# Norm roots taken out of the first FFN products behind two mixers

## The chip, the cores and the metric

The kernel runs on one core of one Trainium2 chip. The metric is device time of one execution in microseconds, median over the timed runs. The engines are TensorE (PE: matmuls; PEld: its weight loads), VectorE (DVE), ScalarE (ACT), GpSimd (POOL) and SyncE (SP, which issues most transfers). Each engine works through its own list of instructions in order.

## The reference

Two layers. Each is half a SwiGLU feed-forward network (FFN), a token mixer (layer 0: a grouped 2-D Fourier transform and a projection; layer 1: retention), and a second half FFN. D is 1024, the FFN is 2816 wide, there are 256 latent and 256 context tokens. Layer 1's mixer updates the latent stream only, so its second FFN has 256 tokens.

```python
def rmsnorm(x, g):
    y = xf * lax.rsqrt(jnp.mean(xf * xf, axis=-1, keepdims=True) + NORM_EPS)
    return (y * g).astype(x.dtype)

def half_ffn(t, m, j):
    h = modulate(rmsnorm(t, norm_g[l, j]), m[3 * j], m[3 * j + 1])   # h * (1 + scale) + shift
    return t + 0.5 * m[3 * j + 2] * swiglu(h, w_gate, w_up, w_down)  # (silu(h @ gate) * (h @ up)) @ down

x = half_ffn(x, m_lat, 0);  ctx = half_ffn(ctx, m_ctx, 0)
y_lat, y_ctx = fourier_layer(...)            # layer 0; retention_layer in layer 1
x = x + m_lat[5] * y_lat;   ctx = ctx + m_ctx[5] * y_ctx
x = half_ffn(x, m_lat, 2);  ctx = half_ffn(ctx, m_ctx, 2)
```

The root of the norm is one number per token; scale and shift are one number per feature.

## The kernel before

Activations stand transposed: features on the 128 partitions, tokens along the row. `x_tile(d, s)` is feature block d (0 to 7) of stream s (0 latent, 1 context), 128x256. To keep float32 precision each operand of a product is a pair, hi (rounded) and lo (the rest); `split` makes it with a cast on ACT (L89) and a subtraction on DVE (L90), and `mm3` issues three matmuls (L132 to L134) for a product. Weight blocks come by DMA as 128x2048 `raw` tiles and are split in two halves (`wh`, `wl`, 128x1024 each), in order, on ACT and DVE.

The FFN works on blocks i of 128 of its 2816 columns: for a block, gate and up each sum 8 products over k (the feature blocks) in one PSUM bank. There are six such banks (`ps`, 128x512). `hidden` evicts a pair: silu on ACT (L437), product on DVE (L439), a split.

Between a mixer and the FFN behind it stands the norm. `square` squares an updated x tile on ACT (L271) and adds it to a running sum (L278: POOL in the Fourier layer, DVE in retention; with `apart=2` the last two tiles are not added). `rstd` sums the sums over the partitions with one-column matmuls (L303), takes the root (ACT L308), its inverse (DVE L310), puts it on a diagonal (L312) and spreads it over the partitions with a matmul (L319). `keep_warm` (L250) issues matmuls whose results are unused, at these points. `norm_mod` then makes the pair of the normed input, per d: x times scale times root on DVE (L335), hi with the shift on ACT (L336), lo on DVE (L337). Only behind these can the FFN's first product start.

In the Fourier layer the last stage (`fourier`, L654 on) goes over the 8 feature blocks d: 24 products plus one matmul of 256 or 258 columns, a copy on ACT (L667), three combinations on DVE (L676 to L678) and the two residual updates of x on DVE (L369), then the squares. `begin_two` starts the FFN that follows with two blocks: latent products of block 0, then of block 1, then the context products of both while norm_mod works on them, and from the third block on the streams go together, 512 columns wide. In retention the last `project_out` ends with the residual updates of the latent tiles, and `begin_narrow` starts the last FFN with blocks 0 and 1, 256 columns wide.

`behind(d)` and `tc.issue_after(x)` only set the order on one engine: what stands in them is put behind the named instruction. All other order on an engine comes from a planner which replays the program with its own durations and lists the instructions by when they would be ready.

Of the kernel before, what the change touches and what calls it, by code (L numbers as in the profile page):

```python
# [16 lines left out]
P = 128  # L17
# [14 lines left out]
GRID_W = 64  # L32


@with_exitstack
def hybrid_block(ctx: ExitStack, tc: tile.TileContext, a: dict, out: bass.AP):
# [44 lines left out]
    def h_tile():  # L81
        return hpool.tile([P, 512], F32R, tag="h", name=nm("h"))
# [170 lines left out]
    sums = {}  # L253

# [13 lines left out]
    def square(d, s, eng=nc.gpsimd, apart=0):  # L268

        sq = q_tile()  # L270
        nc.scalar.activation(sq, x_tile(d, s), AF.Square)  # L271
        if d == 0:
            sums[s] = [sq]
        elif d >= ND - apart:
            sums[s].append(sq)
        else:
            n = q_tile()
            eng.tensor_tensor(n, sums[s][0], sq, ALU.add)  # L278
            sums[s] = [n]
# [44 lines left out]
    def h_tiles():  # L324
        return [(h_tile(), h_tile()) for _ in range(ND)]

    def norm_mod(l, j, s, h, r):
        sl = STREAMS[s]
        done, acts = [], []
        for d in range(ND):  # L330
# [3 lines left out]
            with tc.issue_after(done[d - 3].ins) if d > 2 else nullcontext():  # L334
                nc.vector.scalar_tensor_tensor(u, x_tile(d, s), sc, r, ALU.mult, ALU.mult)  # L335
# [16 lines left out]
    def rstd_tokens():  # L352

        ps = aux_tile()
        for s in range(2):
# [6 lines left out]
        root = spool.tile([P, 4], F32, tag="root4", bufs=1, name=nm("root"))  # L362
        mark[2] = nc.scalar.activation(root, ps[:, :4], AF.Sqrt, bias=epst[:, 1:2])
        inv = spool.tile([P, 4], F32, tag="inv4", bufs=1, name=nm("inv"))
# [64 lines left out]
    def half_ffn(l, j, h, width, begin, after, each=None):  # L429
        f = 2 * l + j // 2  # L430
        off = 0
        for c0, c1 in CHUNKS:
            hid = []

            def hidden(psg, psu):
                sg = t_tile()
                mark[1] = nc.scalar.activation(sg[:, :width], psg[:, :width], AF.Silu)  # L437
                hf = t_tile()
                nc.vector.tensor_tensor(hf[:, :width], psu[:, :width], sg[:, :width], ALU.mult)  # L439
                uh, ul = a_tile(), a_tile()  # L440
                split(uh[:, :width], ul[:, :width], hf[:, :width])
                hid.append((uh, ul))
# [124 lines left out]
    def fourier(l, slot, after):  # L567
# [84 lines left out]
        four["last"] = mark[0], mark[6]  # L652

        for b in range(4):  # L654
# [5 lines left out]
            for d in (2 * b, 2 * b + 1):  # L660
# [18 lines left out]
                for s in range(2):  # L679
                    residual(d, z[:, STREAMS[s]], l, 5, s)  # L680
                    square(d, s, nc.gpsimd, 2)
                    if d == ND - 1 and s == 0:
                        sqrt_table()
                        keep_warm(NW[0], mark[4])
                        after(0)
        after(1)
# [23 lines left out]
    def retention(l, slot, h, mid, after):  # L710
# [220 lines left out]
        def project_out(hd, zt, between=None, behind=None):  # L931
            for half in range(2):
                blk = wblock(a["ret_out"][slot, hd, half], 2048)
                for dd in range(4):
# [7 lines left out]
                    if hd == HEADS - 1:  # L942
                        square(d, 0, nc.vector, 2)
# [4 lines left out]
        for hd in range(HEADS):  # L948
# [39 lines left out]
            else:  # L988
                project_out(hd - 1, zts.pop(0), turn, mark[4].ins)
        project_out(HEADS - 1, zts.pop(0))  # L990
        keep_warm(NW[0], mark[4])
        after(0)
# [11 lines left out]
    def prepare(l, j, width, warm=False):  # L1004
# [16 lines left out]
        return after  # L1021

# [85 lines left out]
    def begin_narrow(load, bank, part, hidden):  # L1108
        blks, banks = [load(0), load(1)], [(bank(), bank()) for _ in range(2)]
        with behind(ND - 1):  # L1110
            pre = [load(2)]
        for k in range(ND):
            for i, gu in ((0, 0), (0, 1), (1, 0)):
                part(blks[i], banks[i][gu], gu, (k,), STREAMS[0])
        part(blks[1], banks[1][1], 1, range(ND), STREAMS[0])
        for i in range(2):
            hidden(*banks[i])
        return 2, pre

# [20 lines left out]
    fourier(0, 0, prepare(0, 2, T2, True))  # L1140
    half_ffn(0, 2, nxt["h"], T2, begin_two, prepare(1, 0, T2))
    half_ffn(1, 0, nxt["h"], T2, begin_two, prepare(1, 1, T2))
    retention(1, 0, nxt["h"], late, prepare(1, 2, S, True))
    half_ffn(1, 2, nxt["h"], S, begin_narrow, finish, scale_out)
# [98 lines left out]
```

## Time and profile before

| | us |
|---|---|
| timed runs, median (lowest to highest of 3) | 1656.64 (1655.84 to 1658.22) |
| the profiled execution, own time | 1658.49 |
| its span, first to last instruction | 1656.7 |
| PE busy in it | 1627.9 |
| DVE busy | 1130.2 |
| ACT busy | 626.8 |
| POOL busy | 122.2 |

Times below are microseconds from the span's start. A row of the time line has start, duration, engine, line, operation, output<-inputs, tile shapes and xcount; in brackets the idle time of the engine ahead of it and what ended it. Matmuls are pipelined, so the distance of two starts is the cost of one, not its duration.

### The profile page before, as it was taken

How to read it: one execution, taken by the hardware profiler on the slowest of the kernel's cores; microseconds unless marked ns; L12 is line 12 of the kernel's file. 1: busy time of each engine (PE TensorE's matmuls, PEld its weight loads, DVE VectorE, ACT ScalarE, POOL GpSimd, SP SyncE). 2: the span in 40 equal slices, each digit the busy share in tenths (PEclk: the TensorE clock that was granted, in tenths of full speed). 3: DMA queues.
4: the chain of work that ended last, by engine and by line, in shares of the span. 5: the costliest groups of instructions: out<-in, count | busy, mean ns of one | idle time of the engine just before them, and what ended most of it. 6: DMA issues, size and time to landing. Idle time of an engine off the chain costs nothing.

```text
span 1656.7 us, 23275 instructions
## 1 busy us (share of the span) xinstructions
PE 1627.9 (98%) x9352; PEld 1422.9 (86%) x9352; DVE 1130.2 (68%) x1805; ACT 626.8 (38%) x910; POOL 122.2 (7%) x192
## 2 busy tenths in 40 slices
PE   6999999999999999999999999999999999999998
PEld 4788888888998888888988888888988999999998
DVE  5588889887866776766567767733666767665554
ACT  4531222345542122223432222233564454354443
POOL 0011011023200000001200000001100000000000
PEclk9999999999999999999999999999999999999999
DMA  9576776752235444544144444522133333345451
GB/s 333 227 269 209 244 258 223 252 189 95 77 140 179 168 165 153 197 162 167 70 153 177 160 161 164 185 90 100 71 127 128 127 112 143 127 165 190 168 189 53
DMA packets 59740, 272.03 MB, mean 164 GB/s; under 512 B 7537, under 2 KB 8945, under 8 KB 41969
## 3 DMA queue, kind: packets, MB, share of 16 engines
q1 hardware_dynamic: 40512, 201.86, 34.5%
q0 software_dynamic: 18576, 68.17, 11.6%
q8 instruction: 73, 1.20, 0.3%
q10 hardware_dynamic: 544, 0.52, 0.1%
q14 instruction: 35, 0.28, 0.1%
HBM read 265.27 MB, written 5.24 MB: 163 GB/s over the span
## 4 chain that ended last, share of the span: by engine, by line
PE 96%; DVE 2%; DMA 1%; ACT 1%; issue 0%; SPq 0%; DVEq 0%; ACTq 0%
PE ps L132 31%; PE ps L133 31%; PE ps L134 31%; DMA a<-in_ada_first 1%; PE ps L764 0%; DMA xctx<-in_x 0%; PE aux L250 0%; PE aux L303 0%; PE aux L195 0%; ACT wh L89 0%; PE aux L319 0%; PE aux L925 0%; DVE a L90 0%; PE ps L839 0%; DVE xlat L369 0%
## 5 line engine op out<-in xcount | busy, mean ns | idle before, releaser
L89 ACT CAST wh<-raw 128x1024 fp32r<-128x1024 f32 x344 | 352.5, 1031 | 713.8 <-PE ps L133 624.0
L133 PE MATMUL ps<-h,wh 128*128 128x512 f32 (+1 forms) x1568 | 556.0, 356 | 0.0
L134 PE MATMUL ps<-h,wl 128*128 128x512 f32 (+1 forms) x1568 | 554.9, 355 | 0.0
L132 PE MATMUL ps<-h,wh 128*128 128x512 f32 (+1 forms) x1568 | 551.1, 356 | 3.6 <-ACT h L89 3.4
L90 DVE TENSOR_TENSOR wl<-raw,wh 128x1024 fp32r<-128x1024 f32 x344 | 410.1, 1197 | 181.2 <-ACT wh L89 177.9
L132 PEld LDWEIGHTS ps<-h,wh 128*128 128x128 f32 x1568 | 294.3, 189 | 46.1 <-ACT h L89 4.0
L133 PEld LDWEIGHTS ps<-h,wh 128*128 128x128 f32 x1568 | 297.1, 190 | 42.1 <-DVE h L90 0.5
L134 PEld LDWEIGHTS ps<-h,wl 128*128 128x128 f32 x1568 | 297.1, 190 | 41.4
L222 DVE CUSTOM_DVE_ANT_0 dump<-araw,wide,adab 128x1024 bf16<-128x1024 f32 x256 | 329.4, 1287 | 3.2
L134 PE MATMUL ps<-a,wl 128*128 128x512 f32 (+2 forms) x952 | 317.5, 336 | 0.0
L132 PE MATMUL ps<-a,wh 128*128 128x512 f32 (+2 forms) x952 | 317.4, 336 | 0.0
L133 PE MATMUL ps<-a,wh 128*128 128x512 f32 (+2 forms) x952 | 317.4, 336 | 0.0
L133 PEld LDWEIGHTS ps<-a,wh 128*128 128x128 f32 x952 | 180.5, 190 | 18.6
L134 PEld LDWEIGHTS ps<-a,wl 128*128 128x128 f32 x952 | 180.5, 190 | 18.4
L132 PEld LDWEIGHTS ps<-a,wh 128*128 128x128 f32 x952 | 179.5, 190 | 18.6
L439 DVE TENSOR_TENSOR t<-ps,t 128x512 f32<-128x512 f32 (+1 forms) x88 | 54.9, 624 | 177.6 <-PE ps L134 149.2
L213 POOL DMA_DIRECT2D araw<-in_ada_w x128 | 67.7, 529 | 828.0 <-DVE mods L222 783.5
L369 DVE SCALAR_TENSOR_TENSOR xlat<-ps,mods,xlat 128x256 f32<-128x256 f32 x128 | 61.1, 481 | 63.6 <-PE ps L134 63.0
L437 ACT ACTIVATE t<-ps 128x512 f32<-128x512 f32 (+1 forms) x88 | 47.9, 545 | 132.7 <-PE ps L134 127.1
L90 DVE TENSOR_TENSOR a<-t,a 128x512 fp32r<-128x512 f32 (+2 forms) x116 | 69.8, 606 | 2.6 <-ACT a L89 2.2
L89 ACT CAST a<-t 128x512 fp32r<-128x512 f32 (+2 forms) x116 | 64.3, 558 | 13.7 <-DVE t L868 9.8
L278 POOL TENSOR_TENSOR q<-q,q 128x256 f32<-128x256 f32 x52 | 46.8, 917 | 177.6 <-ACT q L271 177.1
(208 smaller groups left out, 1142.2 us busy)
## 6 DMA issues: line engine op xcount, KB each, us to landing
raw<-in_wgu SPq DMA_DIRECT2D x85, 1024.0 KB, 4.8
araw<-in_ada_w POOLq DMA_DIRECT2D x128, 512.0 KB, 3.9
raw<-in_wd SPq DMA_DIRECT2D x32, 896.0 KB, 4.5
raw<-in_ret_in SPq DMA_DIRECT2D x24, 1024.0 KB, 4.7
raw<-in_wd SPq DMA_DIRECT2D x16, 1024.0 KB, 4.8
a<-in_ada_first SPq DMA_DIRECT2D x32, 256.0 KB, 5.2
t<-in_four_w SPq DMA_DIRECT2D x32, 256.0 KB, 5.4
raw<-in_ret_out SPq DMA_DIRECT2D x8, 1024.0 KB, 4.7
```

Source lines behind the costliest of these rows:

```text
L89: mark[6] = nc.scalar.copy(hi, src)
L90: i = (lo_eng or nc.vector).tensor_tensor(lo, src, f32(hi), ALU.subtract)
L132: nc.tensor.matmul(ps, lh, rh, start=start, stop=False)
L133: nc.tensor.matmul(ps, lh, rl, start=False, stop=False)
L134: mark[4] = nc.tensor.matmul(ps, ll, rh, start=False, stop=stop)
L213: nc.gpsimd.dma_start(raw, a["ada_w"][l, m, d])
L222: nc.vector.tensor_tensor_reduce(dump, raw, wide[:, v, :], 1.0, adab[:, l, m, d : d + 1], ALU.mult, ALU.add, mods[l][:, m, d, v : v + 1],)
L278: eng.tensor_tensor(n, sums[s][0], sq, ALU.add)
L369: mark[0] = nc.vector.scalar_tensor_tensor(x_tile(d, s), ps, mods[l][:, m, d, s : s + 1], x_tile(d, s), ALU.mult, ALU.add)
L437: mark[1] = nc.scalar.activation(sg[:, :width], psg[:, :width], AF.Silu)
L439: nc.vector.tensor_tensor(hf[:, :width], psu[:, :width], sg[:, :width], ALU.mult)
```

## The change

The FFN behind each mixer starts with products of x times its scale, not of the normed input. The root, one factor per token, is multiplied in when a PSUM bank is evicted (`evict`), and the shift, which the root must not touch, goes through the same matmuls as two extra columns in front of the 256 token columns (`SH = 2`): each h tile is 16 columns longer, and the shift columns stand in columns 14 and 15, the tokens from column 16. `open` fills the shift columns (POOL), `tile(d)` makes the pair of x times scale (ACT, DVE) right behind the latent residual of d, `roots` makes the roots of both streams at once. Behind the Fourier layer block 0 and block 1 of the latent stream are made so (`products`, 258 columns); the context stream and all later blocks take the normed input as before. Behind retention it is blocks 0, 1 and 2. The squares are now all added, all on POOL, and in the Fourier layer they are issued behind both residuals of d, context first. The keep-warm matmuls at both places go. Weight block 1 (behind retention 1 and 2) is split only behind the last `tile` and the last square. All tiles of the pool have the longer form; who else uses them sees them from column 16.

```diff
+SH = 2
+PAD = 16
...
     def h_tile():
-        return hpool.tile([P, 512], F32R, tag="h", name=nm("h"))
+        return hpool.tile([P, PAD + T2], F32R, tag="h", name=nm("h"))
...
-        nc.scalar.activation(sq, x_tile(d, s), AF.Square)
+        squared[0] = nc.scalar.activation(sq, x_tile(d, s), AF.Square)
...
-    def rstd_tokens():
+    def rstd_tokens(n=2, scale=1.0):
         ps = aux_tile()
-        for s in range(2):
+        for s in reversed(range(n)):
...
         four["last"] = mark[0], mark[6]
+        following.open()
...
-                    square(d, s, nc.gpsimd, 2)
-                    if d == ND - 1 and s == 0:
-                        sqrt_table()
-                        keep_warm(NW[0], mark[4])
-                        after(0)
-        after(1)
+                    if s == 0:
+                        following.tile(d)
+                for s in (1, 0):
+                    square(d, s)
+        sqrt_table()
...
-                        square(d, 0, nc.vector, 2)
+                        following.tile(d)
+                        square(d, 0)
...
+        following.open()
         project_out(HEADS - 1, zts.pop(0))
-        keep_warm(NW[0], mark[4])
-        after(0)
...
+    class Ahead:
+        def __init__(self, l, j):
+            self.l, self.j = l, j
+        def open(self):
+            need(self.l, 3 * self.j + 1)
+            self.full = [(h_tile(), h_tile()) for _ in range(ND)]
+            nxt["h"] = [(hi[:, PAD:], lo[:, PAD:]) for hi, lo in self.full]
+            self.full = [(hi[:, PAD - SH :], lo[:, PAD - SH :]) for hi, lo in self.full]
+            nxt["done"] = [], []
+            for d, (hi, lo) in enumerate(self.full):
+                sh = mods[self.l][:, 3 * self.j, d, 0:1].broadcast_to([P, SH])
+                nc.gpsimd.tensor_copy(hi[:, :SH], sh)
+                nc.gpsimd.tensor_tensor(lo[:, :SH], sh, f32(hi[:, :SH]), ALU.subtract)
+        def tile(self, d):
+            sc = mods[self.l][:, 3 * self.j + 1, d, 0:1]
+            hi, lo = (t[:, STREAMS[0]] for t in nxt["h"][d])
+            nxt["done"][1].append(nc.scalar.activation(hi, x_tile(d, 0), AF.Copy, scale=sc))
+            mark[0] = nc.vector.scalar_tensor_tensor(lo, x_tile(d, 0), sc, f32(hi), ALU.mult, ALU.subtract)
+            nxt["done"][0].append(mark[0])
+        def products(self, blk, ps, k):
+            hi, lo = (t[:, : SH + S] for t in self.full[k])
+            for gu in range(2):
+                mm3(
+                    ps[gu][:, : SH + S], wcols(blk, k // 4 * 1024 + gu * 512 + k % 4 * P, P), (hi, lo),
+                    k == 0, k == ND - 1,
+                )
+        def evict(self, ps, r):
+            col = spool.tile([P, 2], F32, tag="col", name=nm("col"))
+            v = []
+            for gu in range(2):
+                nc.vector.tensor_copy(col[:, gu : gu + 1], ps[gu][:, 0:1])
+                v.append(q_tile())
+                nc.vector.tensor_tensor(v[gu], ps[gu][:, SH : SH + S], r, ALU.mult)
+            return v, col
+        def gate(self, v, col, pair):
+            uh, ul = pair
+            sg = q_tile()
+            mark[1] = nc.scalar.activation(sg, v[0], AF.Silu, bias=col[:, 0:1])
+            hf = q_tile()
+            nc.vector.scalar_tensor_tensor(hf, v[1], col[:, 1:2], sg, ALU.add, ALU.mult)
+            split(uh[:, :S], ul[:, :S], hf)
+        def roots(self, n):
+            inv = rstd_tokens(n, 1.0 / D**2)
+            diag = t_tile()[:, : n * S]
+            nc.vector.tensor_tensor(
+                diag.rearrange("p (a b) -> p a b", b=P), ident.unsqueeze(1).broadcast_to([P, 2 * n, P]),
+                inv.unsqueeze(2).broadcast_to([P, 2 * n, P]), ALU.mult,
+            )
+            r = aux_tile()
+            for s in range(n):
+                nc.tensor.matmul(r[:, STREAMS[s]], meanw, diag[:, STREAMS[s]], start=True, stop=True)
+            row = q_tile()
+            nc.scalar.copy(row, r[:, :S])
+            return r, row
+        def begin_two(self, load, bank, part, hidden):
+            late = STREAMS[1]
+            h = nxt["h"]
+            blks, lat = [load(0)], [(bank(), bank()) for _ in range(2)]
+            with behind(ND - 1), tc.issue_after(squared[0].ins):
+                blks.append(load(1))
+            for k in range(ND):
+                self.products(blks[0], lat[0], k)
+                if k == 5:
+                    r, row = self.roots(2)
+            nxt["done"] = norm_mod(self.l, self.j, 1, h, r[:, late])
+            with behind(3):
+                first = self.evict(lat[0], row)
+            for k in range(ND):
+                self.products(blks[1], lat[1], k)
+            with behind(ND - 1):
+                second = self.evict(lat[1], row)
+                pre = [load(2)]
+            ctx = [(bank(), bank()) for _ in range(2)]
+            for k in range(ND):
+                for i in range(2):
+                    for gu in range(2):
+                        part(blks[i], ctx[i][gu], gu, (k,), late)
+                if k == 0:
+                    with tc.issue_after(mark[0].ins), tc.issue_after(mark[6].ins):
+                        nxt["done"] = norm_mod(self.l, self.j, 0, h, r[:, :S])
+            pairs = [(a_tile(), a_tile()) for _ in range(2)]
+            with behind(ND - 1):
+                self.gate(*first, pairs[0])
+                self.gate(*second, pairs[1])
+                for i in range(2):
+                    hidden(*ctx[i], pairs[i], late)
+                pre.append(load(3))
+            return 2, pre
+        def begin_narrow(self, load, bank, part, hidden):
+            n = 3
+            h = nxt["h"]
+            blks, lat = [load(0)], [(bank(), bank()) for _ in range(n)]
+            with behind(ND - 1), tc.issue_after(squared[0].ins):
+                blks += [load(i) for i in range(1, n)]
+            for k in range(ND):
+                self.products(blks[0], lat[0], k)
+                if k == 4:
+                    r, row = self.roots(1)
+            first = self.evict(lat[0], row)
+            h[:] = [(hi[:, S:], lo[:, S:]) for hi, lo in h]
+            with tc.issue_after(mark[0].ins), tc.issue_after(mark[6].ins):
+                nxt["done"] = norm_mod(self.l, self.j, 0, h, r[:, :S], slice(0, S), range(5))
+            with behind(4):
+                pre = [load(n)]
+            with tc.issue_after(mark[0].ins), tc.issue_after(mark[6].ins):
+                done = norm_mod(self.l, self.j, 0, h, r[:, :S], slice(0, S), range(5, ND))
+            nxt["done"] = tuple(i + j for i, j in zip(nxt["done"], done))
+            for i in range(1, n):
+                for k in range(ND):
+                    self.products(blks[i], lat[i], k)
+            with behind(ND - 1):
+                pre.append(load(n + 1))
+                for ready in [first] + [self.evict(ps, row) for ps in lat[1:]]:
+                    pair = a_tile(), a_tile()
+                    self.gate(*ready, pair)
+                    hidden(None, None, pair, None)
+            return n, pre
...
-    fourier(0, 0, prepare(0, 2, T2, True))
-    half_ffn(0, 2, nxt["h"], T2, begin_two, prepare(1, 0, T2))
+    following = Ahead(0, 2)
+    fourier(0, 0, following)
+    half_ffn(0, 2, nxt["h"], T2, following.begin_two, prepare(1, 0, T2))
...
-    retention(1, 0, nxt["h"], late, prepare(1, 2, S, True))
-    half_ffn(1, 2, nxt["h"], S, begin_narrow, finish, scale_out)
+    following = Ahead(1, 2)
+    retention(1, 0, nxt["h"], late, following)
+    half_ffn(1, 2, nxt["h"], S, following.begin_narrow, finish, scale_out)
```

## Rows read from the trace of the kernel before

**Rows 1.** The page: the span, the busy times of TensorE and VectorE with their share of it, and the chain that ended last, by engine.

```profile
span 1656.7 us, 23275 instructions
PE 1627.9 (98%) x9352; PEld 1422.9 (86%) x9352; DVE 1130.2 (68%) x1805; ACT 626.8 (38%) x910; POOL 122.2 (7%) x192
PE 96%; DVE 2%; DMA 1%; ACT 1%; issue 0%; SPq 0%; DVEq 0%; ACTq 0%
```

**Rows 2.** Busy time by stretch: start and end, length, busy time and count of PE, PEld, DVE, ACT, POOL, the granted clock as a share of 2.4 GHz, the DMA share, GB/s. The last stage of the Fourier layer, and the end of retention.

```profile
418.00:443.00 25.00, 25.00 (x211) 25.00 (x210) 22.69 (x48) 14.43 (x31) 9.71 (x10) 1.00 0.35 127
...
1438.00:1457.00 19.00, 18.80 (x156) 18.36 (x155) 13.68 (x26) 9.25 (x17) 0.00 (x0) 1.00 0.43 163
```

**Rows 3.** Time line of PE at the end of retention: the keep-warm matmuls that follow the mixer's last product, the one-column sums, and the FFN's first product.

```profile
1450.70 1.50 PE L250 MATMUL aux<-meanw 128*128 128x128 f32 x12
1452.40 1.47 PE L303 MATMUL aux<-meanw,q 128*128 128x1 f32 x12 [0.19 <-DVE q L278]
...
1456.76 0.73 PE L132 MATMUL ps<-h,wh 128*128 128x256 f32 x4
```

**Rows 4.** Time line of PE behind the Fourier layer: the first of twelve matmuls 256 wide and the first of twelve 258 wide of the last feature block (one more 258 wide stands between the two dozens), the keep-warm matmuls that follow the last of them, the one-column sums, the FFN's first product, the context's sums and spread root inside block 0 and block 1 (with the products next to them), and the first and second matmul 512 wide.

```profile
439.85 0.28 PE L132 MATMUL ps<-a,wh 128*128 128x256 f32 x1
441.41 0.28 PE L132 MATMUL ps<-a,wh 128*128 128x258 f32 x1
442.85 1.50 PE L250 MATMUL aux<-meanw 128*128 128x128 f32 x12
449.03 1.02 PE L303 MATMUL aux<-meanw,q 128*128 128x1 f32 x8
449.91 0.48 PE L132 MATMUL ps<-h,wh 128*128 128x256 f32 x2
452.38 0.50 PE L303 MATMUL aux<-meanw,q 128*128 128x1 f32 x4
452.75 0.36 PE L133 MATMUL ps<-h,wh 128*128 128x256 f32 x1
456.42 0.59 PE L319 MATMUL aux<-q,meanw 128*128 128x256 f32 x2
456.97 0.28 PE L133 MATMUL ps<-h,wh 128*128 128x256 f32 x1
473.88 0.40 PE L132 MATMUL ps<-h,wh 128*128 128x512 f32 x1
474.11 0.40 PE L133 MATMUL ps<-h,wh 128*128 128x512 f32 x1
```

**Rows 5.** Time line of DVE: the residual updates of one feature block in the last Fourier stage, then the combinations and updates of the last block.

```profile
435.13 0.92 DVE L369 SCALAR_TENSOR_TENSOR xlat<-t,mods,xlat 128x256 f32<-128x256 f32 x1
435.97 0.96 DVE L369 SCALAR_TENSOR_TENSOR xctx<-t,mods,xctx 128x256 f32<-128x256 f32 x1
...
443.29 0.41 DVE L676 TENSOR_TENSOR t<-ps,t 128x256 f32<-128x256 f32 x1
444.26 0.48 DVE L369 SCALAR_TENSOR_TENSOR xlat<-t,mods,xlat 128x256 f32<-128x256 f32 x1
444.67 0.48 DVE L369 SCALAR_TENSOR_TENSOR xctx<-t,mods,xctx 128x256 f32<-128x256 f32 x1
```

**Rows 6.** Time line of POOL in the same stage: the adds of the squares, all of them.

```profile
432.61 6.51 POOL L278 TENSOR_TENSOR q<-q,q 128x256 f32<-128x256 f32 x6 [34.13 <-ACT q L271]
439.38 3.31 POOL L278 TENSOR_TENSOR q<-q,q 128x256 f32<-128x256 f32 x4 [0.27 <-ACT q L271]
```

**Rows 7.** Groups of the last Fourier stage and the FFN's start (418 to 466): count, then busy time and mean ns of one, then idle time ahead. The two residual updates, the combinations and the copy of two columns.

```profile
L369 DVE SCALAR_TENSOR_TENSOR xctx<-t,mods,xctx 128x256 f32<-128x256 f32 x8 | 5.3, 657 | 0.0
L369 DVE SCALAR_TENSOR_TENSOR xlat<-t,mods,xlat 128x256 f32<-128x256 f32 x8 | 5.2, 655 | 0.1
L678 DVE COPY t<-ps 128x2 f32<-128x2 f32 x8 | 1.2, 155 | 0.1
```

**Rows 8.** The line that makes the lo part of x times scale in the FFN ahead of the Fourier layer (`scale_parts`): count and the shortest, median and longest ns of one, first and last start; and the ACT line that makes hi.

```profile
L348 DVE SCALAR_TENSOR_TENSOR h<-xlat,mods,h x8: 477/544/1273, 367.4 to 396.4; 128x256 fp32r<-128x256 f32 x8
L347 ACT ACTIVATE h<-xlat,mods x8: 498/510/512, 366.0 to 395.9; 128x256 fp32r<-128x256 f32 x8
```

**Rows 9.** Time line of ACT and DVE behind the two mixers: the last square and four weight casts, two weight remainders; the last residual update of retention.

```profile
444.84 0.42 ACT L271 ACTIVATE q<-xlat 128x256 f32<-128x256 f32 x1 [0.96 <-DVE xlat L369]
453.53 3.87 ACT L89 CAST wh<-raw 128x1024 fp32r<-128x1024 f32 x4
454.59 2.36 DVE L90 TENSOR_TENSOR wl<-raw,wh 128x1024 fp32r<-128x1024 f32 x2
...
1450.90 0.48 DVE L369 SCALAR_TENSOR_TENSOR xlat<-ps,mods,xlat 128x256 f32<-128x256 f32 x1 [0.38 <-PE ps L134]
```

**Rows 10.** Busy time by stretch, columns as in rows 2: a wait of PE at the start of retention and what followed.

```profile
1190.50:1194.00 3.50, 2.37 (x19) 2.08 (x18) 3.50 (x7) 3.50 (x6) 0.00 (x0) 0.97 0.00 0
1194.00:1197.50 3.50, 3.50 (x10) 2.69 (x10) 3.33 (x7) 3.50 (x7) 0.00 (x0) 0.54 0.54 180
```

**Rows 11.** Time line of PE there: two neighbouring matmuls 512 wide.

```profile
1195.56 0.63 PE L133 MATMUL ps<-h,wh 128*128 128x512 f32 x1
1195.98 0.63 PE L134 MATMUL ps<-h,wl 128*128 128x512 f32 x1
```

## What the change should do to the time

> **What bounds the kernel now.** First the page's busy times and its chain: TensorE is busy for 98% of the span and is 96% of the chain that ended last [rows 1]. So time is gained only where PE waits or does work that the result does not need, and a busy PE can hide such work. Next the time line of PE at the two places of the change, since keep-warm matmuls count as busy. At the end of retention the mixer's last product is followed by keep-warm matmuls at 1450.70, and the FFN's first product starts at 1456.76 [rows 3]: 6.06 us in which PE makes one-column sums, one spread root and nothing else that is used. Behind the Fourier layer the same runs from 442.85 to 449.91, 7.06 us [rows 4]. These 13.1 us are all that can be had. Last, the busy times by stretch, to see whether the engines that must deliver earlier have room: DVE is busy 22.69 of the 25 us of the last Fourier stage, but 13.68 of 19 us at the end of retention [rows 2]. The two places therefore have different limits and are summed apart.
>
> **Retention.** Removed: 6.06 us. Added on PE: two token tiles of sums, four one-column instructions. Eight of them take 0.88 us, 449.03 to 449.91 [rows 4], so 0.44. The spread of the root: in the Fourier FFN it stands between two products, 456.42 to 456.97, 0.55 less the one product of 0.12 inside it, 0.43 [rows 4]. Two more columns in 3 x 48 = 144 matmuls: a matmul of 512 columns comes 0.23 after the last, one of 256 0.12, that is 0.43 ns a column and 0.86 ns a matmul, 0.12 us; the 258-wide ones of the Fourier stage, twelve from 441.41 to 442.85, are as close as 256-wide ones, twelve and one more from 439.85 to 441.41 [rows 4], so the bounds are 0 and 0.12 and I take 0.12. Net 6.06 - 0.44 - 0.43 - 0.12 = 5.07 us, if nothing new is waited for.
>
> What could be late: the last residual ends at 1450.90 + 0.48 = 1451.4 [rows 9]; hi on ACT 0.51, lo on DVE about 0.5 [rows 8], so the pair of block 7 is there at 1452.4, and PE, with 42 products of 0.12 ahead, asks for it at 1455.7. The last square follows hi at 1451.9, takes 0.42 [rows 9], and its add on POOL 0.98, the mean of the ten adds in [rows 6]: sums at 1453.3, asked for behind 30 products at 1454.3. This margin of 1.0 us is the smaller one. Weight block 1 is now split behind that square: cast 0.97, remainder 1.18 [rows 9], first half ready at 1454.5, needed at 1457.3. DVE loses six adds and four weight halves ahead of the end and gains eight lo parts, and it had 5 us free [rows 2]. Eviction, gates and norm_mod lie under the 11.6 us of blocks 1 and 2. The shift columns are small POOL instructions before POOL has anything else; I cost them at nothing, and POOL's idle time of 34 us ahead of its adds [rows 6] is their cover. Bounds of the place: 5.2 if the columns are free, about 3 if the sums come 2 us after they are asked for.
>
> **Fourier, work of PE alone.** Removed: 7.06, the context's sums inside block 0 (452.38 to 452.75, 0.37) and its spread root (0.43) [rows 4], together 7.86. Added: eight one-column instructions 0.88, two spread roots 0.86, 96 matmuls x 0.86 ns = 0.08, together 1.82. Net 6.04.
>
> **Fourier, what PE then waits for.** DVE ends the stage at 444.67 + 0.48 = 445.15 [rows 5], with almost nothing spare before [rows 2]. It gains eight lo parts. Their line exists already in the FFN ahead: 0.48 at the shortest, median 0.54, 1.27 at the longest [rows 8]. Undisturbed, two such instructions start 0.41 apart (444.26, 444.67); disturbed, 0.84 (435.13, 435.97) [rows 5]. The disturbed ones run while POOL adds squares, the others behind its last add [rows 5, 6]. So 8 x 0.41 = 3.3 us. To that comes the disturbance: the sixteen updates take 10.5 us where 16 x 0.48 would be 7.7 [rows 5, 7], 2.8 us for ten adds. With fourteen adds it is 1.1 us more at the same rate, and at most 14 x 0.48 - 2.8 = 3.9 more; I take 1.6, near the measured rate, since more instructions are now exposed. DVE ends the stage at 445.15 + 3.3 + 1.6 = 450.0, and the lo part of block 7 at 449.6.
>
> The Trainium skill, "SBUF — State Buffer", section "Who interferes with whom", says that a DVE instruction with two SBUF inputs and a GpSimd instruction that reads SBUF exclude each other for the whole instruction. The trace agrees in kind, 0.92 and 0.96 against 0.48; if every add held up one update, as that rule allows, the stage would end 2.3 us later still.
>
> PE has 42 products before it needs block 7: 442.85 + 42 x 0.12 = 447.9. It waits 1.7 and ends block 0 at 450.3. Weight block 1 is queued behind the last square: updates end 450.0, two squares 0.84, a cast 0.97, a remainder 1.18 [rows 9]: 453.0. In the wait of 2.7 us PE can place the sums: two POOL adds of 0.98 from 450.4 end at 452.4, and with 0.88 of matmuls PE is free at 453.2. Lost: 453.2 - 450.3 - 0.88 = 2.0. Then block 1 and the roots' spread, 5.76 + 0.86, to 459.8. On DVE behind that remainder: the second one 1.18, inverse and diagonal about 0.9 (estimate from two of 0.4), the spread 0.6, four blocks of norm_mod 8 x 0.41, the first eviction 2 x (0.16 + 0.41) [rows 5, 7]: 460.1, when the fourth pair of banks is free. Lost 0.3. So F = 6.04 - 1.7 - 2.0 - 0.3 = 2.0 us; the 512-wide products would start at 471.9, not 473.9 [rows 4].
>
> **The clock.** The keep-warm matmuls are gone. At the start of retention PE was busy 2.37 of 3.5 us, and in the next 3.5 us the granted clock was 0.54 [rows 10]: matmuls 512 wide came 0.42 apart, the 1.2 GHz level, against 0.23 [rows 11, 4]. That cost 3.5 x 0.46 = 1.6 us. The forecast has PE busy for 1.6 of the 5.3 us from 447.9 to 453.2, less than there, so I count 1.6 once: F = 0.4. At the end of retention no wait is forecast, so nothing is counted.
>
> The Trainium skill, "TensorE: Matmul & The Clock Gate", section "Part 1: The HAM clock gate", has the array throttled by default and released by activity. Rows 10 agree; a reading by which short waits never throttle would leave F at 2.0 and the sum at 7.1.
>
> **Sum.** 5.07 + 0.4 = 5.5 us. The profiled execution took 1658.49, 1.8 more than its span and than the median of the runs; it would become 1653.0. The median of 1656.64 becomes 1651.1, and I write 1651.0.
>
> **Rivals.** (1) DVE keeps up in the Fourier stage: the lo parts fall into its free 2.3 us [rows 2] and between the adds. Then F = 6.04 and the time is 1656.6 - 11.1 = 1645.5. For it: the free time; against: the free time lies mostly ahead of the crowded part. (2) The planner lists the sums ahead of products 6 and 7, as the program does (behind k = 5). Then PE stands until the sums are there at 452.4, and 0.88 + 12 x 0.12 follow: block 1 starts at 454.7, 1.5 later, F = -1.1, time 1652.7; with DVE at its upper bound 1654 to 1655. For it: the planner's own durations set the order, and a DVE held up by POOL may not be in them. (3) The wait only moves: sums late at retention too (R = 3) and F at -2.5; 1656. For it: seven adds now on POOL in a row; against: the margin of 1.0. (4) Slower: the new products read their moving tile from column 14, 56 bytes into it, and no row shows a matmul with such a start. If a matmul pays 23 ns for it, 240 of them eat the 5.5 us; at double pace (0.11 more each) it is 26 us, 1677. For it: nothing in the rows; against: the 258-wide matmuls from column 0 cost nothing extra [rows 4]. That the change does nothing is excluded, as both gaps are filled with work that it deletes.
>
> **Chances.** Forecast, 1649 to 1652.5: 0.45. (1) 0.20. (2) 0.20. (3) 0.09. (4) 0.06. The range from 1645.0 to 1655.0 holds the forecast, (1) and nearly all of (2), and leaves out (3) and (4). What can be told from no change is about 0.2%, 3.3 us, so below 1653.3 is faster: 0.45 + 0.20 + 0.12 = 0.77. Same: the rest of (2) and (3), 0.17. Slower: 0.06.
>
> **What would show it.** Retention: the first 258-wide product within 0.2 us of the mixer's last one, no PE wait until block 3. Fourier: DVE's last update near 450, PE waiting before k = 7 and again before block 1 with the cast as releaser, granted clock below 1 in the next few us, first 512-wide matmul at 472 to 474. Pitch of the 258-wide products 0.121; at 0.13 or more rival (4) is at work. The forecast is wrong in its largest doubt if DVE ends the Fourier stage at 447 or at 453.

## The result: 0.3% slower, and where the time went

The changed kernel takes 1662.82 us (median; 1661.85 to 1663.83) where the kernel before takes 1657.60 beside it: ratio 1.0031 [1.0021, 1.0041]. The forecast was 1651. The prediction was wrong, and in sign.

The page of the changed kernel, the lines that answer to [rows 1]:

```profile
span 1660.3 us, 23246 instructions
...
PE 1630.2 (98%) x9264; PEld 1411.4 (85%) x9264; DVE 1140.3 (69%) x1838; ACT 632.2 (38%) x931; POOL 140.8 (8%) x235
...
PE 93%; DVE 3%; DMA 2%; ACT 1%; issue 1%; SPq 0%; POOL 0%; DVEq 0%; ACTq 0%; POOLq 0%
```

PE issues 88 instructions fewer, and is busy 2.3 us longer. No wait explains that: matmuls themselves must have become slower. To find which, four marks on PE's time line cut the span at points that both kernels have. Of the changed kernel: the FFN's first product behind the Fourier layer, the first 512-wide product, the first product behind retention, and the one-column sums behind the last FFN. In this kernel the first and the third follow the mixer's last product directly.

```profile
448.33 0.28 PE L135 MATMUL ps<-h,wh 128*128 128x258 f32 x1
...
476.46 0.40 PE L135 MATMUL ps<-h,wh 128*128 128x512 f32 x1
...
1461.22 0.28 PE L135 MATMUL ps<-h,wh 128*128 128x258 f32 x1
...
1650.73 0.95 PE L307 MATMUL aux<-meanw,q 128*128 128x1 f32 x8
```

The kernel before has its marks in [rows 3, 4] (442.85, 473.88, 1450.70); the last one, from its time line, is this:

```profile
1647.09 0.95 PE L303 MATMUL aux<-meanw,q 128*128 128x1 f32 x8
```

| stretch | before, us | after, us | difference |
|---|---|---|---|
| start to the Fourier layer's last product | 442.85 | 448.33 | +5.48 |
| from there to the first 512-wide product | 31.03 | 28.13 | -2.90 |
| from there to retention's last product | 976.82 | 984.76 | +7.94 |
| from there to the end of the last FFN | 196.38 | 189.51 | -6.87 |
| sum | 1647.09 | 1650.73 | +3.64 |

The change gains at both of its places. It loses more in the first and the third stretch, where the FFNs are that it does not mention. The sum is the difference of the spans (1660.3 - 1656.7 = 3.6).

In those FFNs the time line of PE shows the loss directly. Twelve matmuls on, the kernel before (first pair) is 2.72 us further, 226.7 ns a matmul; the changed one (second pair) 2.77 us, 231 ns:

```profile
599.71 0.39 PE L132 MATMUL ps<-h,wh 128*128 128x512 f32 x1
...
602.43 0.39 PE L132 MATMUL ps<-h,wh 128*128 128x512 f32 x1
```

```profile
599.80 0.39 PE L135 MATMUL ps<-h,wh 128*128 128x512 f32 x1
...
602.57 0.39 PE L135 MATMUL ps<-h,wh 128*128 128x512 f32 x1
```

The groups of PE by shape, 480 to 650 us, show the same as a mean duration (here the mean is of one form, so it can be compared). Before:

```profile
L134 PE MATMUL ps<-h,wl 128*128 128x512 f32 x187 | 72.7, 389 | 0.0
...
L134 PE MATMUL ps<-a,wl 128*128 128x512 f32 x64 | 24.9, 389 | 0.0
```

After:

```profile
L137 PE MATMUL ps<-h,wl 128*128 128x512 f32 x183 | 72.2, 395 | 0.0
...
L137 PE MATMUL ps<-a,wl 128*128 128x512 f32 x64 | 24.9, 389 | 0.0
```

Matmuls that read h went from 389 to 395 ns. Those that read `a` tiles, whose form the change does not touch, stayed at 389, in the same stretch, at the same clock (1.00 from 474 to 1180 us in both kernels). So it is the h tile. Over all matmuls of a kind, the mean distance of starts in the trace is (the pitch, used from here on):

| matmuls that read h | count | before | after |
|---|---|---|---|
| 512 wide, in the three FFNs of 512 tokens | 1056 + 960 + 960 | 226.7 ns | 231.2 ns |
| 256 wide, in the last FFN | 912 | 120.0 ns | 118.3 ns |

2976 x 4.5 ns = 13.4 us lost, and some 0.8 us more on the 192 matmuls 512 wide with which retention reads h (228.8 ns there before, 232.6 after); 912 x 1.7 ns = 1.5 us won. With the two gaps closed by 2.9 and 5.5 us (shown apart below) that makes 13.4 + 0.8 - 1.5 - 8.4 = 4.3 us slower, against 3.6 between the spans. The 0.7 us between them are less than what the first stretch scatters from kernel to kernel (see the clock, below).

### The profile page after: what moved, and what is told of

The parts are those of the page before. It is cut to its first block, busy times and chain, and to the rows that moved or that the text cites. A ratio compares the mean times of both kernels' runs of the same rounds, so it can differ in the third digit from the quotient of the medians.

```text
span 1660.3 us, 23246 instructions
## 1 busy us (share of the span) xinstructions
PE 1630.2 (98%) x9264; PEld 1411.4 (85%) x9264; DVE 1140.3 (69%) x1838; ACT 632.2 (38%) x931; POOL 140.8 (8%) x235
## 4 chain that ended last, share of the span: by engine, by line
PE 93%; DVE 3%; DMA 2%; ACT 1%; issue 1%; SPq 0%; POOL 0%; DVEq 0%; ACTq 0%; POOLq 0%
PE ps L137 31%; PE ps L135 31%; PE ps L136 31%; DMA raw<-in_wgu 1%; DMA a<-in_ada_first 1%; DVE wl L93 1%; PE ps L770 0%; ACT wh L92 0%; DMA xctx<-in_x 0%; DVE xlat L373 0%; PE aux L931 0%; DVE h L1052 0%; PE ps L845 0%; DVE xctx L373 0%; DVE a L93 0%
## 5 line engine op out<-in xcount | busy, mean ns | idle before, releaser
L135 PE MATMUL ps<-h,wh 128*128 128x512 f32 (+2 forms) x1568 | 554.8, 358 | 4.2 <-ACT h L92 3.6
L137 PE MATMUL ps<-h,wl 128*128 128x512 f32 (+2 forms) x1568 | 558.8, 358 | 0.0
L136 PE MATMUL ps<-h,wh 128*128 128x512 f32 (+2 forms) x1568 | 557.6, 357 | 0.8 <-DVE h L1052 0.7
L282 POOL TENSOR_TENSOR q<-q,q 128x256 f32<-128x256 f32 x63 | 57.4, 926 | 214.0 <-ACT q L275 210.4
```

The lines of the kernel that those rows point to most:

```text
L135: nc.tensor.matmul(ps, lh, rh, start=start, stop=False)
L136: nc.tensor.matmul(ps, lh, rl, start=False, stop=False)
L137: mark[4] = nc.tensor.matmul(ps, ll, rh, start=False, stop=stop)
```

## Experiments

**Theory:** the longer h tile makes every 512-wide matmul that reads it slower, and the rest of the change does about what was forecast. **Rival 1:** something in the new code disturbs PE (splits, POOL, the order of weights). **Rival 2:** the chip ran PE differently (clock) in that execution.

### The tile's form alone, and a form that differs

e1_layout is the kernel before with nothing but the longer tile and its columns:

```diff
-        return hpool.tile([P, 512], F32R, tag="h", name=nm("h"))
+        return hpool.tile([P, 528], F32R, tag="h", name=nm("h"))[:, 16:16+512]
```

> The kernel before with nothing but the longer h tiles of the change: 528 columns, tokens from column 16; no shift columns, no new products, the old norm and keep-warm matmuls. Theory A (the layout is the loss): the matmuls 512 wide that read h come 231 ns apart instead of 227, 2976 of them in three FFNs, 13 us; the last FFN's 256-wide ones come 118 apart instead of 120, 1.5 us back; time 1668 to 1670. Theory B (the loss comes from the new work around the FFNs, on the other engines): pitch 227, time 1657 to 1658.

e2_stride keeps the length of 528 but puts the tokens in column 0, to tell the start from the stride:

```diff
+        return hpool.tile([P, 528], F32R, tag="h", name=nm("h"))[:, 0:0+512]
```

> The kernel before with h tiles of 528 columns and the tokens from column 0: the tiles lie 2112 bytes apart instead of 2048, the start inside a tile is as before. Theory A1 (what counts is where the read starts in memory): most tiles still start off the old raster, pitch 229 to 231 for 512 columns, time 1665 to 1669. Theory A2 (what counts is the column inside the tile): pitch 227, time 1657.

l64 is the kernel before with tokens from column 64, 256 bytes into a tile of 2304 bytes (in it, and in all kernels with this tile, the scratch of the table load has one buffer instead of its pool's number):

```diff
+        return hpool.tile([P, 576], F32R, tag="h", name=nm("h"))[:, 64:64+512]
```

> The kernel before with h tiles of 576 columns and the tokens from column 64: every read of 512 columns starts on a multiple of 256 bytes, tiles 2304 bytes apart. Theory A1 with a raster of 256 bytes: pitch back at 227, time 1657. With a raster of 512 bytes or more: pitch 229 to 231, time 1665 to 1669. (The table-load scratch tile has one buffer instead of four, to make room.)

a64 is the changed kernel with that tile:

```diff
-PAD = 16
+PAD = 64
```

> The changed kernel with PAD = 64 instead of 16: tokens from column 64, shift columns in 62 and 63, tiles 2304 bytes apart. If 256 bytes is the raster: 512-wide pitch 227, 13 us less than the changed kernel and 1.5 us of the last FFN given back, 1650 to 1652, faster than both. If the raster is larger: as the changed kernel, 1661 to 1664. If the loss is not the layout (theory B): 1661 to 1664 with pitch 231.

Measured: e1_layout 1669.01 us, ratio 1.0066 [1.0049, 1.0083]; e2_stride 1666.37 and l64 1659.57 (one run each); a64 1650.32, ratio 0.9948 [0.9933, 0.9963]. The group of [rows 4]'s 512-wide form, 480 to 650 us, in e1_layout, e2_stride, l64 and a64, in this order:

```profile
L134 PE MATMUL ps<-h,wl 128*128 128x512 f32 x183 | 72.2, 395 | 0.0
```

```profile
L134 PE MATMUL ps<-h,wl 128*128 128x512 f32 x184 | 72.7, 395 | 0.0
```

```profile
L134 PE MATMUL ps<-h,wl 128*128 128x512 f32 x186 | 72.4, 389 | 0.0
```

```profile
L137 PE MATMUL ps<-h,wl 128*128 128x512 f32 x187 | 72.7, 389 | 0.0
```

The pitches are 231.2 (e1_layout), 230.0 (e2_stride) and 226.7 ns (l64 and a64). So the form alone makes the kernel before 0.66% slower, some 11 us (8 to 14 by the interval), and 13.4 + 0.8 - 1.8 = 12.4 is what the pitches give (its last FFN has 1056 matmuls 256 wide). The third stretch of the table above shows it without the timed runs. From the first 512-wide product to retention's last product e1_layout takes 984.76 us, as the changed kernel does:

```profile
477.19 0.40 PE L132 MATMUL ps<-h,wh 128*128 128x512 f32 x1
...
1461.95 0.38 PE L250 MATMUL aux<-meanw 128*128 128x128 f32 x2
```

Both rivals fall: e1_layout has none of the new code, and l64 and a64 run at the old pitch with a tile that is longer still. The offset of 64 bytes inside the tile is not needed for the loss either: e2_stride has none, but with a stride of 2112 bytes (8 x 256 + 64) each tile starts 64 bytes further against a raster of 256 than the one ahead (raster here: multiples of 256 bytes from where the kernel before has its tiles). With the tile put on 256 bytes the change is 0.52% faster than the kernel before: 8.6 us, where the prediction's sum was 5.5.

### One distance from the raster at a time

phases is the kernel before with the stride of 2304 bytes (9 x 256) and another start in each FFN: tokens from column 16, 32, 48 and 16 (64, 128, 192 and 64 bytes off the raster) in the three FFNs of 512 tokens and in the last one, and from column 64 for retention:

```diff
-        return [(h_tile(), h_tile()) for _ in range(ND)]
+        return [(h_tile()[:, o : o + 512], h_tile()[:, o : o + 512]) for _ in range(ND)]
...
+                nxt["h"] = h = h_tiles({(0, 2): 32, (1, 0): 48, (1, 1): 64, (1, 2): 16}[l, j])
```

> The kernel before with tiles 2304 bytes apart, all tiles of an FFN starting alike: first FFN 64 bytes off the raster of 256, second 128, third 192, retention on it, last FFN (256 wide) 64 off. If any start off 256 costs the same: 512-wide pitch 231 in all three FFNs, time 1669. If a raster of 128 bytes suffices: 231, 227, 231, time 1665. 256-wide pitch in the last FFN 118.

Time 1666.21 us (one run). Time line of PE in each of the three FFNs, twelve matmuls between the rows of a pair: 2.74, 2.80 and 2.80 us.

```profile
99.87 0.39 PE L134 MATMUL ps<-h,wl 128*128 128x512 f32 x1
...
102.61 0.39 PE L134 MATMUL ps<-h,wl 128*128 128x512 f32 x1
...
600.05 0.40 PE L134 MATMUL ps<-h,wl 128*128 128x512 f32 x1
...
602.85 0.40 PE L134 MATMUL ps<-h,wl 128*128 128x512 f32 x1
...
899.97 0.40 PE L134 MATMUL ps<-h,wl 128*128 128x512 f32 x1
...
902.77 0.40 PE L134 MATMUL ps<-h,wl 128*128 128x512 f32 x1
```

Over all of them the pitch is 228.9 ns 64 bytes off, 232.9 at 128 and 233.3 at 192, against 226.7 on the raster. A multiple of 128 bytes is not enough; of 256 is. The four phases average 230.5, and e1_layout and e2_stride, whose tiles go through all four, have 231.2 and 230.0. That these two differ, with the same four starts in another order, says that the start of one read is not the whole price; what else counts stays open. The 256-wide matmuls of the last FFN go the other way: 117.8 ns at 64 bytes off, 120.0 on the raster.

### Each half of the change alone, on the raster

r64 is l64 with the change behind retention only, f64 with the change behind the Fourier layer only:

```diff
-    retention(1, 0, nxt["h"], late, prepare(1, 2, S, True))
-    half_ffn(1, 2, nxt["h"], S, begin_narrow, finish, scale_out)
+    following = Ahead(1, 2)
+    retention(1, 0, nxt["h"], late, following)
+    half_ffn(1, 2, nxt["h"], S, following.begin_narrow, finish, scale_out)
```

> Only the retention half of the change (Ahead behind retention, the Fourier layer and its FFN as before), tokens from column 64. My sum: the gap of 6.06 us goes, 0.99 us of work comes, -5.1 us. Rival (the sums wait for POOL at retention): -3 us or less, with PE waiting at the one-column matmuls.

```diff
-    fourier(0, 0, prepare(0, 2, T2, True))
-    half_ffn(0, 2, nxt["h"], T2, begin_two, prepare(1, 0, T2))
+    following = Ahead(0, 2)
+    fourier(0, 0, following)
+    half_ffn(0, 2, nxt["h"], T2, following.begin_two, prepare(1, 0, T2))
```

> Only the Fourier half of the change (retention and the last FFN as before), tokens from column 64. My sum: DVE ends the Fourier stage about 5 us later, PE waits 4.0 us in all, the first 512-wide matmul comes 2.0 us earlier counted from the last Fourier product, 0.4 with a clock drop. Rival 1 (DVE keeps up): 6.0 us earlier. Rival 2 (sums listed ahead of products 6 and 7): 1.1 us later.

The marks of r64 behind retention, and of f64 behind the Fourier layer:

```profile
1451.67 0.28 PE L135 MATMUL ps<-h,wh 128*128 128x258 f32 x1
...
1642.55 0.50 PE L307 MATMUL aux<-meanw,q 128*128 128x1 f32 x4
```

```profile
444.13 0.28 PE L135 MATMUL ps<-h,wh 128*128 128x258 f32 x1
...
472.29 0.40 PE L135 MATMUL ps<-h,wh 128*128 128x512 f32 x1
```

r64 takes 190.88 us for the last stretch where the kernel before takes 196.38, and l64 196.39: retention is worth 5.50. f64 takes 28.16 where those take 31.03 and 31.02: Fourier is worth 2.87. In each the other place is as before (31.01 and 196.38), and a64 has both (28.17 and 190.88), so they add. In the timed runs r64 is at 0.9974 [0.9963, 0.9985], 4.3 us with the 5.5 inside the interval; f64 at 0.9996 [0.9986, 1.0006], 0.7 us with 2.3 as the end of its interval, so its 2.87 is read from the marks and not confirmed by the times.

### The last FFN alone off the raster

a64n is a64, but the pairs behind retention start in column 16:

```diff
+            pad = PAD if self.l == 0 else 16
```

> The changed kernel with tiles of 576 columns, tokens from column 64, but in the last FFN from column 16 with the normed input from column 272, so its 256-wide reads start 64 bytes off the raster of 256. If 256-wide reads are cheaper off the raster (118.3 ns against 120.0, as the changed kernel showed): 19 blocks x 48 x 1.7 ns = 1.5 us less than with everything on the raster, about 1649. If that came from something else: pitch 120.0 and no gain.

Time 1647.33 us, ratio 0.9943 [0.9927, 0.9959]; the last stretch 188.83 us instead of a64's 190.88. That is 2.05, and 912 x (120.0 - 117.8) ns = 2.0. So the gain of the other sign comes with the start of the read too. It is read from the marks: in the timed runs the intervals of a64 and a64n overlap.

### What holds the Fourier stage

The prediction let the POOL adds hold DVE up. noadds is a64n without the adds of the Fourier layer; the sum of squares there is that of the last tile alone:

```diff
+            else:
+                sums[s] = [sq]
```

> As the kernel with the last FFN off the raster, but POOL adds no squares in the Fourier layer: only the last feature block's square is used for the roots behind it, so the roots are wrong numbers; everything else is computed. It shows what the adds cost DVE. My sum had 4.4 us of hold-up on DVE in this stage, 2.8 of it already there before: DVE's last update, 3.95 us behind the last Fourier product on PE with the adds, should come at about 0 to 1. If the adds hardly hold DVE up: 3 to 4, and the eight lo parts are the whole delay.

a64r is a64n with the matmuls that spread the root listed behind the third feature block of weight block 1 (18 of its 48 products), instead of behind 38 of them:

```diff
+                with tc.issue_after(mark[7].ins) if k > 2 else nullcontext():
+                    self.products(blks[1], lat[1], k)
```

> As the kernel with the last FFN off the raster, and the two matmuls that spread the roots are listed on PE behind the third of the eight feature blocks of block 1, not where the planner put them. If their place in PE's list is what delays the context's norm (DVE stood idle 4.3 us ahead of it): norm_mod of the context starts 2 to 2.5 us earlier, PE no longer waits among the context products, and the first 512-wide matmul comes 1.0 to 1.6 us earlier, 26.6 to 27.2 us behind the last Fourier product instead of 28.2. If the context products wait for something else: 28.2.

Time line of DVE, last residual update, in the changed kernel, in a64n and in noadds (there with the wait ahead of its last combinations):

```profile
452.28 0.48 DVE L373 SCALAR_TENSOR_TENSOR xctx<-t,mods,xctx 128x256 f32<-128x256 f32 x1
```

```profile
445.44 0.48 DVE L373 SCALAR_TENSOR_TENSOR xctx<-t,mods,xctx 128x256 f32<-128x256 f32 x1
```

```profile
442.44 0.42 DVE L688 TENSOR_TENSOR t<-ps,t 128x256 f32<-128x256 f32 x1 [1.39 <-PE ps L137]
...
444.50 0.48 DVE L377 SCALAR_TENSOR_TENSOR xctx<-t,mods,xctx 128x256 f32<-128x256 f32 x1
```

The first matmul behind the Fourier layer's last product starts at 448.33, 441.49 and 442.17 in these; DVE's last update ends 4.4, 4.4 and 2.8 us behind that (kernel before: 2.3, [rows 4, 5]). In all three two lo parts follow the last update and are the end of DVE's work for the stage. In the changed kernel and in noadds:

```profile
452.68 1.83 DVE L1052 SCALAR_TENSOR_TENSOR h<-xlat,mods,h 128x256 fp32r<-128x256 f32 x2
```

```profile
444.89 0.87 DVE L1059 SCALAR_TENSOR_TENSOR h<-xlat,mods,h 128x256 fp32r<-128x256 f32 x2
```

They end 6.2 us behind the Fourier layer (in a64n too), and 3.6 in noadds. So the adds cost the updates 1.6 us and the whole of DVE's stage 2.6, where the sum had 4.4; without them DVE catches up and stands 1.39 us for PE, so part of what they hold up was time that it had free. Without them, and with its eight lo parts, it ends 1.3 later than in the kernel before, which has ten adds. The last update starts 2.3 us behind the Fourier layer, between the two values expected. The stretch to the first 512-wide product is 25.94 instead of 28.18; in noadds the sums also stand earlier in PE's list, inside block 0, so these 2.2 us are not the adds' alone. The time is 1645.36 us (one run).

a64r shows the other half of the loss. Its spread, then a64n's:

```profile
453.94 1.02 PE L1092 MATMUL aux<-t,meanw 128*128 128x256 f32 x4
```

```profile
454.59 1.02 PE L1092 MATMUL aux<-t,meanw 128*128 128x256 f32 x4
```

That is 10.7 instead of 13.1 us behind the Fourier layer's last product (443.23 and 441.49), and the stretch is 26.64 instead of 28.18. The time, 1645.15 us (one run), does not tell the two apart: a64n's four runs lie between 1645.1 and 1649.8. In a64n, as in the changed kernel, the norm of the context waited for that spread.

### The best of it

best is a64r, and the hidden tiles of the last FFN too stand 64 bytes off the raster, since its down products are 256 wide:

```diff
+                if width == S and pair is None:
+                    uh, ul = uh[:, 16:], ul[:, 16:]
...
-                    pair = a_tile(), a_tile()
+                    pair = a_tile()[:, 16:], a_tile()[:, 16:]
```

> All that helped: tokens from column 64, last FFN off the raster, spread of the roots listed earlier, and the hidden tiles of the last FFN from column 16, so that its down products, 528 matmuls 256 wide, read off the raster too. Pitch of these 118 instead of 120: 1.2 us; with the earlier spread 1.3 us: 2.5 us less than without both, 1644 to 1646, ratio to the kernel before 0.992 to 0.993. If the reads off the raster are no cheaper for these tiles: 1645 to 1647.

Time 1643.95 us, ratio 0.9917 [0.9904, 0.9931]: the fastest of all. Groups of the last FFN by shape, 1490 to 1630 us, first before, then best:

```profile
L134 PE MATMUL ps<-a,wl 128*128 128x256 f32 x128 | 36.0, 283 | 0.0
```

```profile
L137 PE MATMUL ps<-a,wl 128*128 128x256 f32 x169 | 46.9, 280 | 0.0
```

The down products came to 117.8 ns, 528 of them, and the last stretch to 187.65: 1.18 less than a64n, where 528 x 2.2 ns is 1.16.

## Why the prediction was wrong

**The step that failed** is the change part by part: the tile's new form was read as a matter of the shift columns alone. The description of the change above says that all tiles of the pool have the longer form, and the sum has no term for the other matmuls that read them. There are 2976 of 512 columns in the FFNs and 192 in retention. The forecast gain of 5.5 us was gone at 1.9 ns on each of the 2976, 0.8% of a pitch, and no row of the kernel before showed a read with another start, so nothing excluded that. The measured term is 13.4 + 0.8 - 1.5 = 12.7 us.

**Rival (4)** had the right resource, the start of the moving read, at the wrong matmuls. It looked at the 240 new ones and needed 23 ns on each. Those cost next to nothing: 36 of them in the changed kernel, from 448.33 to 452.70, are 121.4 ns apart, where the prediction gave 120.9 for two more columns. The few ns that decide were on the many matmuls that the diff does not touch.

**Retention** was right. First product directly behind the mixer's last, no wait of PE up to the spread, as forecast; 5.50 us measured with the form undone, 5.07 forecast. Of the 0.43 between them some 0.2 are the new products, 119.3 ns apart in a64 instead of 120.9; the rest is open. PE in the changed kernel, from ahead of the first product (1461.22) to near the end of the last FFN, columns as in [rows 2]:

```profile
1457.00:1640.00 183.00, 183.00 (x1538) 182.95 (x1537) 117.63 (x175) 95.51 (x143) 5.62 (x7) 1.00 0.47 168
```

**Fourier** was right in what PE waits for, and wrong in the order of DVE's work and so in two sizes. PE waits for a lo part (that of feature block 6, behind 38 products; the forecast had block 7) and for the sums, but short. The waits of PE from 440 to 480 us:

```profile
PE ps L136 <- DVE h L1052: 0.7, 1, 0.7
PE aux L362 <- POOL q L282: 0.5, 1, 0.5
PE ps L135 <- ACT h L340: 0.4, 1, 0.4
```

0.7 stands against 1.7, and 0.5 against 2.0. DVE's end of stage, with all eight lo parts, was not far off: 6.2 us behind the mixer's last product (452.68 + 1.83 - 448.33) instead of 7.15. Lo parts and more adds were to move that end by 3.3 + 1.6 = 4.9 us; they moved it by 3.9, and no run separates the two terms. The larger part is the order. The forecast had the last update at the end; the planner put two lo parts behind it, and the last update ends 4.4 us behind the mixer. So the squares and the casts of weight block 1 came earlier: the first cast starts at 453.51, 5.2 us behind the mixer's last product, where the forecast had 8.0. In what was forecast as an empty wait for the sums PE has the context's sums and four products of block 1 to do, and it does not wait for the cast at all. The cast on ACT, then PE:

```profile
453.51 1.98 ACT L92 CAST wh<-raw 128x1024 fp32r<-128x1024 f32 x2
...
455.21 0.56 PE L362 MATMUL aux<-meanw,q 128*128 128x1 f32 x4
455.63 0.37 PE L135 MATMUL ps<-h,wh 128*128 128x258 f32 x1
...
456.82 0.61 PE L362 MATMUL aux<-meanw,q 128*128 128x1 f32 x4 [0.47 <-POOL q L282]
```

Rival (1), DVE keeps up, did not come: in the changed kernel DVE waits for nothing from 430 to 454.5 us, so each lo part pushes what stands behind it. Part of the gain was given back by a wait that nobody forecast. DVE, in the changed kernel:

```profile
454.57 3.28 DVE L93 TENSOR_TENSOR wl<-raw,wh 128x1024 fp32r<-128x1024 f32 x2
457.78 0.17 DVE L369 RECIPROCAL inv<-root 128x4 f32<-128x4 f32 x1
457.98 0.69 DVE L1085 TENSOR_TENSOR t<-ident,inv 128x512 f32<-128x512 f32 x1
462.98 1.26 DVE L339 SCALAR_TENSOR_TENSOR q<-xctx,mods,aux 128x256 f32<-128x256 f32 x3 [4.31 <-ACT q L1093]
```

The diagonal is there at 458.7, the context's norm_mod starts at 462.98: in between DVE stands, because the spread is listed behind 38 of the 48 products of block 1. By a64r this cost 1.5 us. In all, 6.04 - 2.87 = 3.2 us were lost behind the Fourier layer, where the forecast had 1.7 + 2.0 + 0.3 = 4.0 ahead of the clock; with 1.5 of the 3.2 at a place that it did not have, the nearness of the two is luck in part. Rival (2), which had products of block 0 behind the sums, did not come.

The weight remainders beside POOL's adds took 3.28 us where [rows 9] have 2.36. The Trainium skill, "SBUF — State Buffer", section "Who interferes with whom", has a DVE instruction with two SBUF inputs and a GpSimd instruction that reads SBUF exclude each other. The trace agrees for the single instruction: in noadds, without the adds, the same two remainders take 2.36.

```profile
446.77 2.36 DVE L93 TENSOR_TENSOR wl<-raw,wh 128x1024 fp32r<-128x1024 f32 x2 [1.00 <-ACT wh L92]
```

For the stage noadds gives 2.6 us for fourteen adds.

**The clock** term of 1.6 did not come either. Windows behind the Fourier layer in the changed kernel, and the one stretch near it that does have a lower clock:

```profile
443.00:457.00 14.00, 12.85 (x104) 12.37 (x103) 13.90 (x29) 8.02 (x19) 9.78 (x11) 1.00 0.15 63
```

```profile
419.00:423.00 4.00, 2.71 (x13) 2.50 (x14) 3.87 (x17) 2.30 (x8) 0.00 (x0) 0.75 0.00 0
```

With waits this short PE was busy 12.85 of 14 us, and the clock stayed full without keep-warm matmuls. The drop at 419 to 423 is in front of the last Fourier stage, and not the change's: l64, which has none of it, shows 0.82 from 415 to 418. The kernel before had its own at 1194 to 1197.5 [rows 10], where the changed one has 1.00. That trades places within the table above, for some 1.6 us each (the estimate of the prediction's clock term): more in its first line, less in its third. The first line also scatters by itself: the last one-column sum ahead of the Fourier layer stands between 398.7 and 401.6 us in the kernels that read on the raster, and at 405.3 in the changed one.

## What to carry to other kernels

A new layout for a tile is a change to every instruction that reads it. Count all its readers first, divide the forecast gain by that count, and ask whether any row excludes a loss of that size on each; here 4.5 ns on 2976 matmuls outweighed two real gains of 5.5 and 2.9 us. When a change adds columns in front of a tile, keep the wide readers where they were against 256 bytes, which took one constant and a smaller scratch pool here and turned 0.3% slower into 0.5% faster. And when busy time rises while instructions fall, compare one form of one instruction in one stretch before looking for waits.

## What the runs showed that was not expected

- A 512-wide matmul of these operands has a pitch of 226.7 ns when its moving read starts on the raster of 256 bytes, 228.9 at 64 bytes off, 232.9 at 128 and 233.3 at 192.
- A 256-wide one is slower on the raster: 120.0 ns, against 117.8 at 64 bytes off, for h and for `a` tiles alike. Why the sign turns with the width stays open; no run tells it.
- Between 100 and 1640 us stretches at a lower clock come at places that differ from kernel to kernel (near 1194 us before, near 421 after, near 417 and 1195 in l64, none in a64n), each some 1 to 2 us dear (estimate, from the granted clock as in [rows 10]). Marks on the time line of one engine made gains of 1 to 5 us readable in spite of that.
